# Moving the expert-row gathers of a transformer block along the routing: a pace for each of its five phases

## Chip, cores and metric

The kernel runs on one core of a Trainium2 chip. The metric is the device time of one execution in microseconds (us). The kernel before takes 3159.07 us in the median of 3 runs (3156.07 to 3160.61). The core has five engines with a queue each: PE (TensorE, matrix products), DVE (VectorE), ACT (ScalarE), POOL (GpSimd) and SP (SyncE, which here only issues DMAs). DMAs are issued by SP, ACT and POOL, each on a queue of its own (q1, q10 and q0 in the profile), and 16 DMA engines move the data of all of them.

## What is computed

The reference is two blocks on 512 tokens of width 1024, in float32. The part that matters here is the feed-forward of the first block, in which every token picks its experts out of 16384:

```
q  = (t @ wq) split into 8 heads x 2 halves of 128
s  = q . sub_keys                      # 8 heads x 2 x 128 scores per token
s1, i1 = top16(s[:, :, 0]);  s2, i2 = top16(s[:, :, 1])
cand = s1[:, None] + s2[None, :]       # 16 x 16 per head
top, pos = top16(cand);  idx = i1 * 128 + i2 at pos
g = softmax(top)
a = gelu(u[idx] . t)                   # 8 heads x 16 experts per token
out = sum over the 128 picks of (g * a) * v[idx]
```

Ahead of it stands a mixer (neighbourhood attention and a gated linear recurrence), and behind it the second block (short convolution, attention, two dense feed-forwards). Neither is touched.

## The kernel before

**Two ways through the feed-forward.** The 512 tokens are four tiles of 128. Tiles 1 to 3 (`dense`, 384 tokens) are computed over all 16384 experts, as 128 "experts" of 128 rows each: `hidden` makes `gelu(U_e . t)` for a whole e with 24 matmuls of 384 columns; `products` multiplies with V, 18 matmuls of 512 columns per e, after `operands` has multiplied the hidden values by the weights `Wr` that the routing gave (zero where an expert isn't picked). Tile 0 goes another way: its 128 picks per token are fetched row by row. A gather (L1135) is an indirect DMA that POOL issues: 128 rows of 1024 floats, one for each token, into a tile `gr`, of which there are five (`GBUFS`). For the tables U and V together there are 256 of them. On a row of U, DVE makes the dot product with the token (`gr`, L1154); on a row of V it adds weight times row to `accg` (L1157 once, then L1159). After 16 dot products ACT makes their gelu (L1161) and DVE the weights `wt` (L1162). A gather is issued `GAHEAD` = 3 gathers ahead of the row that DVE works on.

**The stage of the routing** (716 to about 1305 us). In `peer`, three lists of work are woven (L1046):

- `route`: in five phases. In phases 0 to 3 `topk` finds the top 16 for one token tile, on DVE alone (L1230 to L1234, L1271 to L1274). In phases 2 to 4 `spread` makes the dense weights of tiles 1 to 3: DVE compares (`oh`, `go`, L1313), ACT scales, PE multiplies the one-hots (`spread_mm`), ACT writes them out to `Wd` in DRAM. In phases 2 and 3 the two are merged.
- `ahead`: the hidden values of the first 112 experts, each with a load of U by SP, a split by ACT (`wh`, L1341) and DVE (`wl`, L1342), the 24 matmuls on PE, and a write of the result to `Ad` in DRAM. The other 4 of `AHEAD` = 116 follow behind the routing, the last 12 in the products.
- `until_routed(gather)`: once tile 0 has its experts (`choose`, at the end of phase 0), pairs of gathers. A pair is one of U and one of V from the second head on.

`weave` gives each list a clock of its own: what a list yields is the time in us that its last piece is taken to last, and the list whose clock is behind goes next. `route` yields 1.0 for a search, 1.45 for a piece of `spread` and so on, some 330 in all; `ahead` yields `PACE` = 2.95 an expert; a pair of gathers yields `GATHER` = 11.0 (L1164). PE's order is kept as woven (`manual_schedule`); the orders of the other engines come from the scheduler, which takes the woven order as its start. The rows on gathered tiles are placed behind the last search or spread piece woven so far (`self.after(self.anchor)`).

**The stage of the products with V** (about 1322 to 1960 us). What is left of the 129 pairs (`gather_left`, L1121), 103, is dealt out evenly to the first 120 experts (L1062 and following). For each expert SP loads V (`w`, L1374) and the hidden values (`act`, L1367), and once in 8 experts (`GROUP`) the weights `Wr` of eight experts (L1364, in runs of 512 bytes). DVE multiplies (`act`, L1371) and splits (`sl`, `vl`, L135), ACT splits (`sh`, `vh`, L133), and PE runs its 18 matmuls two experts behind (`OPS_LAG`). There are 3 tiles of `act`, 2 of `Wr` and 4 of `w`.

All engines work their queues in order. A row of DVE that waits for its gather holds everything behind it on DVE.

Of the kernel before, what the change touches and what calls it, by code (L numbers as in the profile page):

```python
# [29 lines left out]
WT = 16  # L30
GBUFS = 5
GAHEAD = 3
GATHER = 11.0
OPS_LAG = 2
TAIL = 2
STATE = 3.0
# [39 lines left out]
def merge(*gens):  # L76

    at = [[0.0, i, g] for i, g in enumerate(gens)]
    out = [None] * len(gens)
    while at:  # L80
        cur = min(at, key=lambda x: (x[0], x[1]))
        try:
            d = next(cur[2])
            cur[0] += d
            yield d
        except StopIteration as e:
            out[cur[1]] = e.value
            at.remove(cur)
    return out


class Net:
# [1030 lines left out]
    def gathered(self, pg, ac):  # L1123


        nc, p = self.nc, self.p
        iu, iv, g = self.chosen
        dots = ac.tile([128, 8, 16], F32, name="dots")
        wt = ac.tile([128, 8, 16], F32, name="wt")
        self.accg = acc = ac.tile([128, D], F32, name="accg")  # L1130
        ring = {}

        def load(key, table, idx):
            ring[key] = t = pg.tile([128, D], F32, name="gr", bufs=GBUFS)
            nc.gpsimd.indirect_dma_start(out=t, out_offset=None, in_=table, in_offset=bass.IndirectOffsetOnAxis(ap=idx, axis=0))  # L1135

        jobs = []
        for h in range(9):
            for k in range(16):
                if h < 8:  # L1140
                    jobs.append(("u", h, k))
                if h:
                    jobs.append(("v", h - 1, k))
        for n in range(len(jobs) + GAHEAD):
            if n < len(jobs):
                what, h, k = jobs[n]
                i = h * 16 + k
                load(n, p['Un'] if what == "u" else p['V'].rearrange("a b d -> (a b) d"), (iu if what == "u" else iv)[:, i:i + 1])
            if n >= GAHEAD:
                what, h, k = jobs[n - GAHEAD]  # L1150
                t = ring.pop(n - GAHEAD)
                with self.after(self.anchor):
                    if what == "u":
                        nc.vector.scalar_tensor_tensor(t, t, 1.0, self.h0, op0=OP.mult, op1=OP.mult,  # L1154
                                                       accum_out=dots[:, h, k:k + 1])
                    elif h == k == 0:
                        nc.vector.tensor_scalar(acc, t, wt[:, h, k:k + 1], None, op0=OP.mult)  # L1157
                    else:
                        nc.vector.scalar_tensor_tensor(acc, t, wt[:, h, k:k + 1], acc, op0=OP.mult, op1=OP.add)  # L1159
                if what == "u" and k == 15:  # L1160
                    nc.scalar.activation(wt[:, h], dots[:, h], AF.Gelu)  # L1161
                    nc.vector.tensor_tensor(out=wt[:, h], in0=wt[:, h], in1=g[:, h], op=OP.mult)  # L1162
            if n % 2:
                yield GATHER  # L1164

    def queries(self, mv, first):

# [31 lines left out]
    def route(self, pq, pg, sc):  # L1199
        nc = self.nc  # L1200
        self.io = io = pq.tile([128, 128], F32, name="io")
        nc.gpsimd.iota(io, pattern=[[1, 128]], base=0, channel_multiplier=0, allow_small_or_imprecise_dtypes=True)
        self.routing = True
        cur = None
        for t in range(5):
            gens = []
            if t < 4:
                gens.append(self.topk(pq, sc[t], io))
            if t > 1:
                gens.append(self.spread(pq, t - 1, *cur, io))  # L1210
            cur = (yield from merge(*gens))[0]
            if t == 0:
                self.choose(pg, *cur)
        self.routing = False
# [616 lines left out]
```

## Time and profile before

| | us |
|---|---|
| median of 3 runs | 3159.07 |
| range of the runs | 3156.07 to 3160.61 |
| the profiled execution, its own time | 3161.74 |
| its span in the trace | 3159.9 |

| engine | busy us | share of the span |
|---|---|---|
| PE | 2967.1 | 94% |
| DVE | 1900.2 | 60% |
| ACT | 1268.5 | 40% |
| POOL | 472.1 | 15% |

The DMA engines move 170 GB/s in the mean over the span. The shares are means over very different stages, so the profile is read stage by stage: for each stretch the busy time of each engine, the granted clock of PE (1.00 is its full speed of 2.4 GHz, the other level is 1.2 GHz), the mean busy share of the 16 DMA engines and what they moved. An engine whose busy time fills a stretch bounds it; DMA bounds it where its share stands at 1.0. Matmuls are pipelined, so the distance of their starts, not their own duration, is what one costs. The rows themselves follow in a section of their own.

### The profile page before, as it was taken

Reading aid. Unit: us, or ns where it says so; the run is one execution under the profiler, and the core shown is the slowest. Engines: PE = TensorE matmul, PEld = TensorE weight load, DVE = VectorE, ACT = ScalarE, POOL = GpSimd, SP = SyncE. Lnnn points to the kernel's source line nnn. Section 1 sums busy time; section 2 is a strip of 40 time slices with the busy share of each in tenths; the row PEclk is TensorE's granted clock in tenths of the full one; section 3 lists DMA queues with packets and bytes.
Section 4 is the critical chain, followed back from the end, with each engine's and each line's share of the span. In section 5 each row is a group of like instructions: output and inputs, shape, how many; then the busy total and the mean of one; then the engine's idle time right before and its main releaser. Section 6 shows DMA issues by size and latency. Waiting matters only on the chain.

```text
span 3159.9 us, 42417 instructions
## 1 busy us (share of the span) xinstructions
PE 2967.1 (94%) x16073; PEld 2540.5 (80%) x16073; DVE 1900.2 (60%) x3614; ACT 1268.5 (40%) x2275; POOL 472.1 (15%) x464
## 2 busy tenths in 40 slices
PE   7999889999999999898898888899999999999998
PEld 5887787799899999777776767778888887788887
DVE  5744487539999856588788885544333235533323
ACT  4233464343376677532223323432433234433222
POOL 2101332000111111043344441000000000000000
PEclk9999899999999999999999999999999999999999
DMA  6622202235766766799999996223333322133332
GB/s 245 230 61 75 62 1 71 97 114 162 233 218 235 252 229 234 270 356 365 356 348 349 365 360 225 67 74 97 94 96 94 100 87 68 48 92 95 94 106 80
DMA packets 257165, 537.79 MB, mean 170 GB/s; under 512 B 20160, under 2 KB 135104, under 8 KB 252608
## 3 DMA queue, kind: packets, MB, share of 16 engines
q1 hardware_dynamic: 196512, 345.82, 33.9%
q0 software_dynamic: 36864, 134.23, 12.1%
q10 hardware_dynamic: 23584, 55.03, 4.6%
q8 instruction: 126, 2.06, 0.3%
q14 instruction: 79, 0.65, 0.1%
HBM read 484.93 MB, written 50.08 MB: 169 GB/s over the span
## 4 chain that ended last, share of the span: by engine, by line
PE 58%; DVE 18%; DMA 8%; issue 3%; ACT 1%; POOL 1%; SPq 0%; DVEq 0%; ACTq 0%; POOLq 0%
PE bank L122 56%; DMA act<-Ad 6%; DVE wl L1342 2%; DVE accg L1159 2%; DVE gr L1154 2%; DVE vl L135 2%; DVE sl L135 1%; DVE act L1371 1%; PE bank L606 1%; PE bank L1470 1%; DVE idx L1274 1%; DVE tmp L1232 1%; DVE eq L1271 1%; DVE eq L1273 1%; DVE go L1313 1%
## 5 line engine op out<-in xcount | busy, mean ns | idle before, releaser
L122 PE MATMUL bank<-hh,wl 128*128 128x512 f32 (+2 forms) x2304 | 839.2, 365 | 45.9 <-DVE wl L1342 32.2
L122 PE MATMUL bank<-hh,wh 128*128 128x512 f32 (+2 forms) x2304 | 843.6, 367 | 15.1 <-ACT wh L1341 5.3
L122 PE MATMUL bank<-hl,wh 128*128 128x512 f32 (+2 forms) x2304 | 833.0, 362 | 1.1 <-DVE hl L272 0.6
L149 DVE TENSOR_TENSOR wl<-w,wh 128x1024 fp32r<-128x1024 f32 (+2 forms) x280 | 303.4, 1084 | 651.5 <-ACT wh L148 643.8
L148 ACT ACTIVATE wh<-w 128x1024 fp32r<-128x1024 f32 (+2 forms) x280 | 257.4, 920 | 751.7 <-PE bank L122 609.9
L122 PEld LDWEIGHTS bank<-hh,wl 128*128 128x128 f32 x2304 | 438.4, 190 | 106.0 <-DVE wl L1342 42.6
L122 PEld LDWEIGHTS bank<-hh,wh 128*128 128x128 f32 x2304 | 438.0, 190 | 66.7 <-ACT wh L1341 6.1
L122 PEld LDWEIGHTS bank<-hl,wh 128*128 128x128 f32 x2304 | 438.6, 190 | 50.5 <-DVE hl L530 1.4
L122 PE MATMUL bank<-vh,sh 128*128 128x512 f32 x768 | 249.6, 407 | 43.6 <-ACT sh L133 24.5
L1135 POOL DMA_INDIRECT gr<-in_Un_dram,iu x128 | 165.9, 1296 | 738.7 <-DVE accg L1159 496.6
L122 PE MATMUL bank<-vl,sh 128*128 128x512 f32 x768 | 251.6, 410 | 19.2 <-DVE vl L135 19.0
L122 PE MATMUL bank<-vh,sl 128*128 128x512 f32 x768 | 247.1, 404 | 0.0
L133 ACT ACTIVATE sh<-act 128x384 fp32r<-128x384 f32 x128 | 67.1, 525 | 383.0 <-DVE act L1371 346.5
L122 PEld LDWEIGHTS bank<-vh,sh 128*128 128x128 f32 x768 | 150.5, 198 | 79.3 <-ACT sh L133 27.4
L1342 DVE TENSOR_TENSOR wl<-w,wh 128x1024 fp32r<-128x1024 f32 x128 | 155.8, 1219 | 77.4 <-ACT wh L1341 77.4
L1341 ACT ACTIVATE wh<-w 128x1024 fp32r<-128x1024 f32 x128 | 134.9, 1055 | 165.1 <-PE bank L122 142.3
L122 PEld LDWEIGHTS bank<-vl,sh 128*128 128x128 f32 x768 | 150.7, 199 | 58.6 <-DVE vl L135 27.3
L122 PEld LDWEIGHTS bank<-vh,sl 128*128 128x128 f32 x768 | 151.3, 197 | 33.5 <-DVE sl L135 0.3
L1135 POOL DMA_INDIRECT gr<-in_V_dram,iv x128 | 150.2, 1174 | 175.7 <-DVE gr L1154 107.3
L216 POOL TENSOR_TENSOR r<-r,mhalf 128x1 f32<-128x1 f32 x37 | 21.8, 591 | 1026.5 <-DVE r L215 1019.8
L135 DVE TENSOR_TENSOR vl<-w,vh 128x1024 fp32r<-128x1024 f32 x128 | 156.3, 1221 | 12.7 <-ACT vh L133 12.3
L1159 DVE SCALAR_TENSOR_TENSOR accg<-gr,wt,accg 128x1024 f32<-128x1024 f32 x127 | 162.4, 1279 | 0.0
(375 smaller groups left out, 4889.8 us busy)
## 6 DMA issues: line engine op xcount, KB each, us to landing
w<-in_U_dram SPq DMA_DIRECT2D x128, 512.0 KB, 4.6
w<-in_V_dram SPq DMA_DIRECT2D x128, 512.0 KB, 7.1
w<-in_wgu_dram SPq DMA_DIRECT2D x84, 512.0 KB, 3.7
Wd<-W ACTq DMA_DIRECT2D x24, 1024.0 KB, 6.7
Wr<-Wd SPq DMA_DIRECT2D x16, 1536.0 KB, 17.9
w<-in_wdown_dram SPq DMA_DIRECT2D x44, 512.0 KB, 3.6
Ad<-act ACTq DMA_DIRECT2D x116, 192.0 KB, 3.8
act<-Ad SPq DMA_DIRECT2D x116, 192.0 KB, 6.8
```

The source lines that it names most:

```text
L122: return self.nc.tensor.matmul(out, a, b, start=start, stop=stop)
L133: self.nc.scalar.activation(hi, src, AF.Copy)
L135: (low or self.nc.vector).tensor_tensor(out=lo, in0=src, in1=hi, op=OP.subtract)
L148: self.nc.scalar.activation(hi[:, :, :n], w[:, :, :n], AF.Copy)
L149: (self.low or self.nc.vector).tensor_tensor(out=lo[:, :, :n], in0=w[:, :, :n], in1=hi[:, :, :n], op=OP.subtract)
L606: nc.tensor.matmul(o, x[k], y[:, kk, :256], start=k == 0 and i == 0 and t % 2 == 0, stop=k == KC - 1 and i == 2, skip_group_check=True)
L1135: nc.gpsimd.indirect_dma_start(out=t, out_offset=None, in_=table, in_offset=bass.IndirectOffsetOnAxis(ap=idx, axis=0))
L1154: nc.vector.scalar_tensor_tensor(t, t, 1.0, self.h0, op0=OP.mult, op1=OP.mult, accum_out=dots[:, h, k:k + 1])
L1159: nc.vector.scalar_tensor_tensor(acc, t, wt[:, h, k:k + 1], acc, op0=OP.mult, op1=OP.add)
L1232: nc.vector.match_replace(tmp, val[:, 0:8], src, -3e38)
L1341: nc.scalar.activation(uh, w, AF.Copy)
L1342: nc.vector.tensor_tensor(out=ul, in0=w, in1=uh, op=OP.subtract)
```

## The change

`GATHER` becomes a table of five numbers, one for each phase of `route`, and `route` writes the number of the phase that it is in to `self.phase`. A pair of gathers so counts 14.0 in phases 0 and 1 (in which none or the first of them run), 11.0 in phase 2, as before, 4.3 in phase 3 and 1.7 in phase 4.

```diff
-GATHER = 11.0
+GATHER = (14.0, 14.0, 11.0, 4.3, 1.7)
...
             if n % 2:
-                yield GATHER
+                yield GATHER[self.phase]
...
         self.routing = True
         cur = None
         for t in range(5):
+            self.phase = t
             gens = []
```

`gather_left` becomes 69 of 129 pairs, dealt out to the same 120 experts. No instruction is added or taken away. Two places show what moves; in both listings the names are those of the part above, and lines of the kernel after stand one number higher behind the added line.

DVE at the end of the routing, from the 102nd expert's `wl` to the next one, before:

```order
L1342 TENSOR_TENSOR wl<-w,wh 128x1024
L1313 TENSOR_TENSOR oh<-io,eT 128x512
L1313 TENSOR_TENSOR go<-io,eT 128x512
L1313 TENSOR_TENSOR oh<-io,eT 128x512
L1313 TENSOR_TENSOR go<-io,eT 128x512
L1159 SCALAR_TENSOR_TENSOR accg<-gr,wt,accg 128x1024
L1154 SCALAR_TENSOR_TENSOR gr,dots<-gr,h_5526 128x1024
L1313 TENSOR_TENSOR oh<-io,eT 128x512
L1342 TENSOR_TENSOR wl<-w,wh 128x1024
```

and after, between the same two:

```order
L1343 TENSOR_TENSOR wl<-w,wh 128x1024
L1159 SCALAR_TENSOR_TENSOR accg<-gr,wt,accg 128x1024
L1162 TENSOR_TENSOR wt<-wt,gw 128x16
L1154 SCALAR_TENSOR_TENSOR gr,dots<-gr,h_5526 128x1024
L1314 TENSOR_TENSOR oh<-io,eT 128x512
L1314 TENSOR_TENSOR go<-io,eT 128x512
L1159 SCALAR_TENSOR_TENSOR accg<-gr,wt,accg 128x1024
L1154 SCALAR_TENSOR_TENSOR gr,dots<-gr,h_5526 128x1024
L1314 TENSOR_TENSOR oh<-io,eT 128x512
L1314 TENSOR_TENSOR go<-io,eT 128x512
L1343 TENSOR_TENSOR wl<-w,wh 128x1024
```

Where one expert in four had a pair of rows on gathered tiles, an expert now has two to four such rows between its `wl` and the next.

DVE in the products, from the 62nd product of `act` and `Wr` on, before:

```order
L1371 TENSOR_TENSOR act<-act,Wr 128x384
L1159 SCALAR_TENSOR_TENSOR accg<-gr,wt,accg 128x1024
L135 TENSOR_TENSOR sl<-act,sh 128x384
L135 TENSOR_TENSOR vl<-w,vh 128x1024
L1154 SCALAR_TENSOR_TENSOR gr,dots<-gr,h_5526 128x1024
L1371 TENSOR_TENSOR act<-act,Wr 128x384
```

and after:

```order
L1372 TENSOR_TENSOR act<-act,Wr 128x384
L135 TENSOR_TENSOR sl<-act,sh 128x384
L135 TENSOR_TENSOR vl<-w,vh 128x1024
L1372 TENSOR_TENSOR act<-act,Wr 128x384
L1159 SCALAR_TENSOR_TENSOR accg<-gr,wt,accg 128x1024
L135 TENSOR_TENSOR sl<-act,sh 128x384
L135 TENSOR_TENSOR vl<-w,vh 128x1024
L1154 SCALAR_TENSOR_TENSOR gr,dots<-gr,h_5526 128x1024
L1372 TENSOR_TENSOR act<-act,Wr 128x384
```

Of the experts in the products nearly all had a pair, and now about two in three have one. PE's order in the routing is the same in both kernels.

## Rows read from the trace of the kernel before

**Rows 1.** the page, slices of 79 us: busy tenths of DVE and of DMA.

```profile
DVE  5744487539999856588788885544333235533323
...
DMA  6622202235766766799999996223333322133332
```

**Rows 2.** busy time by stage, all instructions; the first line names the columns.

```profile
core 0: us, PE busy (x) PEld busy (x) DVE busy (x) ACT busy (x) POOL busy (x), PEclk, DMA share, GB/s
715.80:1035.50 319.70, 301.48 (x1783) 294.73 (x1782) 318.49 (x1095) 171.33 (x301) 38.32 (x28) 0.99 0.65 213
1035.50:1115.10 79.60, 77.19 (x485) 76.13 (x484) 67.14 (x89) 55.97 (x114) 14.68 (x10) 1.00 0.75 253
1115.10:1196.90 81.80, 81.80 (x522) 81.80 (x521) 46.88 (x58) 57.89 (x110) 10.47 (x8) 1.00 0.74 250
1196.90:1304.50 107.60, 102.49 (x642) 97.18 (x641) 69.11 (x96) 87.47 (x194) 10.47 (x8) 1.00 0.63 220
...
1330.00:1900.00 570.00, 503.88 (x2048) 404.56 (x2049) 461.59 (x635) 165.40 (x227) 227.90 (x192) 0.92 1.01 357
```

**Rows 3.** the same stages, instructions of line L1342 alone, one for each expert.

```profile
715.80:1035.50 319.70, 77.71 (x64) 0.99 0.65 213
1035.50:1115.10 79.60, 18.24 (x15) 1.00 0.75 253
...
1196.90:1304.50 107.60, 19.50 (x17) 1.00 0.63 220
```

**Rows 4.** DVE in order of time: start us, us, instruction; 1127 to 1131 us.

```profile
1127.68 1.28 DVE L1159 SCALAR_TENSOR_TENSOR accg<-gr,wt,accg 128x1024 f32<-128x1024 f32 x1
1128.88 1.22 DVE L1154 SCALAR_TENSOR_TENSOR gr<-gr,h 128x1024 f32<-128x1024 f32 x1
1130.02 0.08 DVE L1154 DVE_READ_ACCUMULATOR gr<-gr,h 128x1 f32 x1
```

**Rows 5.** DMA queues from 1330 to 1900 us: packets, MB, share of 16 engines.

```profile
q0 software_dynamic: 27648, 100.68, 48.4%
```

**Rows 6.** SP's queue in order of time: start us, us to issue.

```profile
1516.93 0.38 SPq L1364 DMA_DIRECT2D Wr<-Wd  x1
1518.60 12.17 SPq L1367 DMA_DIRECT2D act<-Ad  x1
```

**Rows 7.** DVE in order of time; in brackets the idle time before and its releaser.

```profile
1537.92 0.56 DVE L1371 TENSOR_TENSOR act<-act,Wr 128x384 f32<-128x384 f32 x1 [8.24 <-DMA act<-Ad]
```

**Rows 8.** what DVE waited for, 1330 to 1900 us: us in total, times, longest.

```profile
DVE act L1371 <- DMA act<-Ad: 101.5, 16, 8.9
```

**Rows 9.** landing of `Wr`, from the view of that tile.

```profile
DMA to landing us min/median/max: 7.5/17.9/20.5
```

**Rows 10.** PE in order of time around one of these waits.

```profile
1534.16 0.62 PE L122 MATMUL bank<-vl,sh 128*128 128x512 f32 x2
1534.61 0.61 PE L122 MATMUL bank<-vh,sl 128*128 128x512 f32 x2
1539.14 0.73 PE L122 MATMUL bank<-vh,sh 128*128 128x512 f32 x2 [3.92 <-ACT sh L133]
...
1541.16 1.05 PE L122 MATMUL bank<-vh,sh 128*128 128x512 f32 x2
1542.01 1.05 PE L122 MATMUL bank<-vl,sh 128*128 128x512 f32 x2
```

**Rows 11.** gathers (L1135) over the span: duration ns min/median/max, and landing.

```profile
L1135 POOL DMA_INDIRECT gr<-in_Un_dram,iu x128: 939/1014/2149, 781.2 to 1874.7; - x128
...
DMA to landing us min/median/max: 4.1/7.3/10.2
```

**Rows 12.** the page, DMA issues: count, KB each, median us to landing.

```profile
w<-in_V_dram SPq DMA_DIRECT2D x128, 512.0 KB, 7.1
...
Wr<-Wd SPq DMA_DIRECT2D x16, 1536.0 KB, 17.9
...
act<-Ad SPq DMA_DIRECT2D x116, 192.0 KB, 6.8
```

## The prediction, as it went on record

> **What bounds the kernel now.** I read the forty slices first, then the busy time by stage, then the rows inside the two stages that the change touches. In the slices [rows 1] DVE is near 9 in the tenth to fourteenth slice, and DMA stands at 9 from the eighteenth to the twenty-fourth. So the routing and the products with V, one behind the other, have different limits. The table by stage [rows 2] cuts the routing where the 1st, 65th, 80th and 96th expert's `wl` comes (counts in [rows 3]; one record seems to be missing there, so a boundary may be off by one expert).
>
> - 716 to 1036 us (64 experts): DVE is busy 318.49 of 319.70 us. It is full; PE gets 301 us of work done beside it, so it only just waits. DMA is at 0.65.
> - 1036 to 1115 us (16 experts): DVE 67.14 of 79.60, PE 77.19. DVE has 12.5 us left.
> - 1115 to 1197 us (16 experts): PE is full, DVE has 34.9 us left, DMA stands at 0.74.
> - 1197 to 1304.5 us (16 experts, with the last token tile's one-hots, 64 `oh` and `go` rows): PE 102.49 of 107.60; DVE has 38.5 us left and DMA 0.37 of the stretch. This is the loosest place of the routing.
> - 1330 to 1900 us, the products: DMA is busy 1.01 of the time at 357 GB/s, PE 504 of 570 at a granted clock of 0.92, DVE 462. DMA is the bound.
>
> The rows inside the products say how the full DMA reaches PE. SP issues the next `Wr` (1536 KB [rows 12], once in 8 experts) at 1516.9 us, and the `act` behind it takes 12.17 us to issue [rows 6]. DVE, done at 1529.7, stands until 1537.9 for that `act` [rows 7]. There are 16 such waits, 101.5 us in all [rows 8]. Their source is the landing of `Wr`, 17.9 us in the median [rows 9, 12] but 7.5 at best [rows 9]: it queues behind other traffic. PE, two experts behind, then stops for 3.92 us and afterwards runs at the lower of its two clock levels: two matmuls 0.85 us apart instead of 0.45 [rows 10].
>
> **The change part by part.** PE's order in the routing stays as it was. Only the gathers move. Counted in the two orders of DVE, its rows on gathered tiles are, before and after: ahead of the 65th expert's `wl` 23 and 24; up to the 81st 10 and 22; up to the 97th 8 and 19; up to the 113th 8 and 52; behind that 207 and 139. Each such row is one gather of 128 rows of 4 KB (0.524 MB) on POOL's queue and one pass of DVE. The passes cost 1.20 and 1.14 us from start to start [rows 4], 1.17 us in the mean.
>
> *A gather's price on the DMA engines.* In the products POOL's queue q0 took 48.4% of 16 engines' 570 us [rows 5] for the 192 gathers that POOL issued there [rows 2]: 275.9 / 192 = 1.44 us of all engines for one.
>
> *The products.* 68 gathers leave; 192 of 207 fall into the stretch, so 63 of them there, 63 x 1.44 = 91 us of DMA. The DMA work of the stretch goes from 1.01 x 570 = 576 us to 485. PE has 2048 matmuls [rows 2] at 0.455 us for two [rows 10], 466 us: still under 485, so DMA stays the bound, with only 4% between the two. DVE, at 462, loses 63 x 1.17 = 74. Bounds: 485 if DMA stays full (-85); 466 if PE alone set the end (-104); 538 if only some 40% of the DMA relief is used, because the `Wr` comes in bursts and DMA then idles between them (-32). I take 500, that is DMA busy 97% of the time, because with 0.91 of the time asked for between the bursts there is little room for idling: an expert takes 0.52 MB of V, 0.20 of `act` [rows 12] and 1.15 gathers (138 over 120 experts), 1.32 MB in eighteen matmuls' 4.1 us, or 324 of the 357 GB/s. **-70 us.**
>
> *Routing up to the 81st expert.* 13 gathers more on DVE, 13 x 1.17 = 15.2 us, against 1.2 + 12.5 = 13.7 us that DVE had free. At least 1.5 us is lost. At most all 15, as the order also puts a part of the last search some six experts later (its end moves from the 78th `wl` to the 84th; what it feeds is transposed by PE ahead of the 97th, so that wait isn't reached). I take **+5**. The 'few beside the first searches' is worth nothing on balance: 24 against 23 rows by the 65th expert.
>
> *81st to 97th expert.* 11 gathers more: 12.9 us of DVE against 34.9 free, 15.8 us of DMA against 0.26 x 81.8 = 21.3 free. **0**; if the cover is gone, up to 15.
>
> *97th to 113th expert.* 44 gathers more. DVE: 69.1 + 44 x 1.17 = 120.6 us against a stretch of 107.6, so +13 from DVE alone. DMA: 0.63 x 107.6 = 67.8, plus 44 x 1.44 = 63.4, makes 131 us, +23.6. DMA becomes the bound, at the very place where the loosest stretch was. Behind a late gather DVE's in-order queue holds the `wl` of the next expert, for which PE waits, and `oh`/`go`, for which PE's one-hot products wait. I take DMA's figure and a little for gathers that come late although DMA is full: **+25**, between +13 and +63 (rival B). This stretch gives back part of what the products gain.
>
> *What is beside it.* The last experts, the 12 whose first product is made late, see 5 gathers less or more at most: 0. SP's own list of loads is the same, in nearly the same order. POOL had 38.32 us of work in 319.7 in the densest DVE stretch, 1.37 us a gather [rows 2]; 52 of these are 71 us in a stretch of 131.
>
> *Sum.* -70 + 5 + 0 + 25 = -40 us. The profiled execution took 3161.7 us, so 3121.7 there; that run lies 2.7 us above the median of the runs shown, 3159.07, so I forecast **3119 us**.
>
> **A rule weighed.** In the stretch where DVE was full a gather took POOL 1.37 us, in the products 1.19 [rows 2], and the longest on U's table 2.15 [rows 11]: the issue does get slower beside a busy DVE, and the crowded stretch has DVE busy throughout. What a slow issue costs there is worked out from these rows as rival B. The Trainium skill, SBUF — State Buffer, section 'SBUF: two separate sides', says that DMAs issued from GpSimd's queue are starved while DVE runs certain operations, since the descriptors can't be written through the locked port; its example grows from about 620 to 3100 ns. By that figure the 52 gathers of the crowded stretch would keep POOL busy for an estimated 161 us, the stretch would cost 53 us in place of 25, and the kernel would end near 3147. The trace shows the direction of that rule, but no gather on U's table as slow as its example.
>
> **The rivals.**
>
> *A. The waits for `Wr` are a matter of lead, not of load (slower).* SP is about three `act` ahead of DVE, 12.8 us from the issue of `Wr` (1516.9) to the point at which DVE needs it (1529.7). If `Wr` and the `act` behind it still land some 18 us later, the same stop stands at each group of 8 experts, PE runs 8 x 4.1 = 33 us and stops as before, and the products give back nothing. Then only the routing's cost is left: +30, **3189 us**. It decides against the change as soon as less than 30 of the 91 us come back, that is if a group of 8 (about 41 us) shortens by under 2 us. For it: these waits sit at one place per group. Against it: `Wr` can land in 7.5 us, and DMA's 1.01 leaves no doubt that it queues.
>
> *B. The five buffers of the gather ring set the pace of the crowded stretch (no change).* A buffer's round is the pass on DVE, the issue and the landing; with the longest in the trace, 1.28 [rows 4] + 2.15 + 10.2 us [rows 11], a round is 13.6 us, 2.7 us a gather, 141 us for 52. While DVE stands for one it does none of its other 60 us (`wl` and one-hot rows: 69.1 of [rows 2] less 8 gathers' 9.4); if half of that isn't hidden, the stretch takes 171, +63. With -70 and +5: -2, **3157 us**. Against it: the medians, 1.01 and 7.3 us, give 1.9 us a gather, 100 us.
>
> *C. DMA stays full and nothing else is lost.* Products -85, crowded stretch +13 since writes of `Wd` and `Ad` can lag, the rest 0: -72, **3087 us**.
>
> That the change doesn't do what it says can be set aside: the order shows 52 gathers where 8 were, and 139 behind.
>
> **How the numbers follow.** The forecast's own case 0.62 (it runs from 3089, products -85 and routing +15, to 3149, products -55 and routing +45), A 0.12, B 0.08, C 0.18. About 0.2% (6 us) is what a measurement of this kernel can tell from no change. Faster by more: 0.62 + 0.18 = 0.80; within: 0.08; slower: 0.12. The range goes from below C, at 3070 (products at PE's 466 us, -104, with +13 to +15 in the routing), up to 3158 with B, and leaves A out.
>
> **What would show it.** In the new profile: the stretch of the last 16 experts of the routing grows from 107.6 to some 130 us, with DMA at 0.95 or more and DVE waiting for gathers; DVE's waits on `act<-Ad` in the products fall from 101.5 us to under 50, the median landing of `Wr` falls from 17.9 us to under 15, the granted clock of the products rises above 0.92, and the stage takes about 500 us. The prediction is wrong if the products keep their stops of some 40 us spacing (A), if the crowded stretch takes over 150 us (B), or if it isn't longer at all (then the sum lacks a cover that I don't see).

## The result, and the profile after

The change makes the kernel slower. It takes 3240.27 us in the median (3233.27 to 3256.14), the kernel before 3159.84 in the same comparison (3156.07 to 3161.09): 1.026 times as long, 95% interval 1.0231 to 1.0288. The forecast was 3119 us; the sign is wrong. The profiled execution, the fastest of its four, has a span of 3231.2 us, 71.3 more than before.

The forty slices of the page, DVE and DMA, answer to [rows 1]:

```profile
DVE  5744396549999879766666666544433235543323
...
DMA  6622102236676789988878888313233231123332
```

DMA stood at 9 through the products with V before. Now it stands at 8: no engine is full in them, and still they take longer. The table by stage says the same in numbers. Each stretch runs from the start of one expert's `wl` to that of another (1st, 65th, 81st, 97th, 113th), the last from the 9th to the 113th product of `act` and `Wr`. The columns are those of [rows 2]. After:

```profile
692.10:1022.20 330.10, 313.52 (x1898) 306.83 (x1896) 314.41 (x1081) 179.28 (x316) 38.37 (x30) 0.99 0.63 209
1022.20:1125.00 102.80, 90.02 (x518) 88.07 (x519) 89.81 (x159) 61.20 (x118) 28.74 (x20) 0.92 0.73 253
1125.00:1207.30 82.30, 79.73 (x508) 79.41 (x508) 64.61 (x87) 56.01 (x109) 29.01 (x21) 1.00 0.86 312
1207.30:1336.00 128.70, 110.09 (x651) 104.36 (x650) 119.17 (x161) 91.51 (x195) 66.28 (x52) 0.95 0.97 368
...
1387.90:1971.20 583.30, 486.62 (x1940) 384.23 (x1939) 366.27 (x495) 155.25 (x216) 140.90 (x121) 0.93 0.83 276
```

The same stretches of the kernel before, without the first one:

```profile
1024.80:1112.50 87.70, 85.30 (x521) 84.23 (x522) 75.83 (x104) 59.51 (x118) 14.68 (x10) 0.98 0.73 243
1112.50:1191.50 79.00, 79.00 (x505) 79.00 (x504) 46.88 (x58) 56.02 (x108) 10.47 (x8) 1.00 0.73 248
1191.50:1303.30 111.80, 106.69 (x666) 101.38 (x666) 69.18 (x95) 89.22 (x196) 10.47 (x8) 1.00 0.64 223
...
1358.10:1890.60 532.50, 469.72 (x1903) 376.32 (x1903) 430.60 (x589) 156.63 (x215) 213.68 (x180) 0.92 1.01 357
```

The routing costs 35 us more (15 + 3 + 17), about what was forecast. The products, from which 70 us were to go, cost 51 us more. DVE has 64 us less to do there and moves less data (276 GB/s in place of 357). What DVE waits for in that stretch, after (total us, times, longest), and PE:

```profile
DVE act L1372 <- DMA act<-Ad: 212.5, 81, 9.4
...
PE bank L122 <- DVE vl L135: 96.6, 45, 5.4
```

What SP's queue waits for, from 1380 to 1960 us, in the same columns:

```profile
SPq L1368 <- DVE sl L135: 292.7, 82, 8.7
```

The same of the kernel before, from 1358 to 1890 us:

```profile
SPq L1367 <- DVE sl L135: 162.8, 54, 11.2
```

In [rows 8] DVE waited 16 times, 101.5 us in all; 12 of these waits, 91 us, stand at the third expert of a group of eight, whose `act` SP issues right behind a `Wr`. Now it waits at four experts out of five: 89 us at the first expert of a group, where the `act` behind a `Wr` now stands, and 124 us at the other seven. In both kernels DVE's work and its waits for `act` make up nearly the whole stretch: 430.6 + 101.5 of 532.5 us before, 366.3 + 212.5 of 583.3 after. So the change took 64 us of work from DVE there and gave it 111 us of waiting. Yet the loads themselves have become quicker. The landing of `Wr`, from that tile's view, against [rows 9]; and the page's DMA issues, against [rows 12]:

```profile
DMA to landing us min/median/max: 7.8/10.0/13.6
```

```profile
w<-in_V_dram SPq DMA_DIRECT2D x128, 512.0 KB, 5.3
...
act<-Ad SPq DMA_DIRECT2D x116, 192.0 KB, 4.8
```

`Wr` lands in 10.0 us in place of 17.9, V in 5.3 in place of 7.1, `act` in 4.8 in place of 6.8. So the `act` is not slow, it is asked for too late, and SP's row says why: SP waits for DVE's `sl`. It did so before too, but then the load still left well ahead of its use. A tile of `act` is free when its last reader, `sl`, is done; there are three tiles, so the load for expert k + 3 can't go out before the `sl` of expert k. One such load in time, after, DVE's queue and then SP's:

```profile
1508.86 0.55 DVE L135 TENSOR_TENSOR sl<-act,sh 128x384 fp32r<-128x384 f32 x1
...
1512.01 0.56 DVE L1372 TENSOR_TENSOR act<-act,Wr 128x384 f32<-128x384 f32 x1 [0.33 <-DMA act<-Ad]
1512.49 0.55 DVE L135 TENSOR_TENSOR sl<-act,sh 128x384 fp32r<-128x384 f32 x1
...
1518.26 0.56 DVE L1372 TENSOR_TENSOR act<-act,Wr 128x384 f32<-128x384 f32 x1 [4.09 <-DMA act<-Ad]
```

```profile
1509.43 0.33 SPq L1368 DMA_DIRECT2D act<-Ad  x1
...
1513.07 0.33 SPq L1368 DMA_DIRECT2D act<-Ad  x1
```

The `sl` ends at 1509.41, the load leaves at 1509.43, and the very next product, at 1512.01, is the one that needs it. The next `sl` ends at 1513.04, the load leaves at 1513.07, and DVE stands 4.09 us for it. The same place before:

```profile
1509.08 0.55 DVE L135 TENSOR_TENSOR sl<-act,sh 128x384 fp32r<-128x384 f32 x1
...
1511.93 0.56 DVE L1371 TENSOR_TENSOR act<-act,Wr 128x384 f32<-128x384 f32 x1
...
1516.35 0.56 DVE L1371 TENSOR_TENSOR act<-act,Wr 128x384 f32<-128x384 f32 x1
...
1520.76 0.56 DVE L1371 TENSOR_TENSOR act<-act,Wr 128x384 f32<-128x384 f32 x1
```

```profile
1509.66 0.32 SPq L1367 DMA_DIRECT2D act<-Ad  x1
```

Here the load of 1509.66 serves the third product behind it, at 1520.76: a lead of 11 us in place of 2.6. These two are typical: matched load by load from the 9th to the 113th product, the time from the issue of an `act` to the point at which DVE is ready for it is 11.0 us in the median before and 2.6 after. The difference stands in DVE's order. With the numbers of the tiles, at the place that the section on the change showed without them, before (left out: the rows on gathered tiles and `vl`):

```
L1371 TENSOR_TENSOR act_15206<-act_15206,Wr_15025 128x384
L135 TENSOR_TENSOR sl_15211<-act_15206,sh_15209 128x384
L1371 TENSOR_TENSOR act_15243<-act_15243,Wr_15025 128x384
L135 TENSOR_TENSOR sl_15248<-act_15243,sh_15246 128x384
```

and after:

```
L1372 TENSOR_TENSOR act_15310<-act_15310,Wr_15135 128x384
L135 TENSOR_TENSOR sl_15241<-act_15236,sh_15239 128x384
L1372 TENSOR_TENSOR act_15341<-act_15341,Wr_15135 128x384
L135 TENSOR_TENSOR sl_15278<-act_15273,sh_15276 128x384
L1372 TENSOR_TENSOR act_15378<-act_15378,Wr_15135 128x384
L135 TENSOR_TENSOR sl_15315<-act_15310,sh_15313 128x384
```

Before, a product is followed by its own `sl`. After, the `sl` of `act_15310` stands behind the products of the next two experts. Counted over the 128 experts: before, 118 `sl` stand behind their own product and 10 behind the next one; after, 16, 42 behind the next and 70 behind the one after that. Each place that `sl` falls back is a tile of lead lost, and with two of three lost a load goes out only just ahead of its use.

### The profile page after: what moved, and what is told of

It is laid out like the page before. It is cut to its first block, busy times and chain, and to the rows that moved or that the text cites. A ratio compares the mean times of both kernels' runs of the same rounds, so it can differ in the third digit from the quotient of the medians.

```text
span 3231.2 us, 42528 instructions
## 1 busy us (share of the span) xinstructions
PE 2984.2 (92%) x16073; PEld 2551.6 (79%) x16073; DVE 1904.6 (59%) x3614; ACT 1267.6 (39%) x2275; POOL 473.1 (15%) x464
## 4 chain that ended last, share of the span: by engine, by line
PE 52%; DVE 18%; DMA 14%; issue 4%; POOL 1%; ACT 1%; SPq 0%; DVEq 0%; POOLq 0%; ACTq 0%
PE bank L122 50%; DMA act<-Ad 10%; DVE accg L1159 3%; DMA gr<-in_Un_dram,iu 2%; DVE wl L1343 2%; DVE gr L1154 2%; DVE sl L135 1%; DVE vl L135 1%; DVE oh L1314 1%; PE bank L606 1%; PE bank L1471 1%; DVE go L1314 1%; DMA Ad<-act 1%; DVE KX L801 1%; DVE QX L802 1%
## 5 line engine op out<-in xcount | busy, mean ns | idle before, releaser
L1135 POOL DMA_INDIRECT gr<-in_Un_dram,iu x128 | 174.0, 1360 | 732.1 <-DVE accg L1159 472.7
L1372 DVE TENSOR_TENSOR act<-act,Wr 128x384 f32<-128x384 f32 x128 | 71.1, 559 | 227.4 <-DMA act<-Ad 220.8
L1342 ACT ACTIVATE wh<-w 128x1024 fp32r<-128x1024 f32 x128 | 135.1, 1056 | 166.6 <-PE bank L122 145.9
L1135 POOL DMA_INDIRECT gr<-in_V_dram,iv x128 | 149.6, 1169 | 245.8 <-DVE accg L1159 138.1
L216 POOL TENSOR_TENSOR r<-r,mhalf 128x1 f32<-128x1 f32 x37 | 21.8, 590 | 1028.4 <-DVE r L215 1021.6
```

The source lines that it names most:

```text
L1342: nc.scalar.activation(uh, w, AF.Copy)
L1372: self.anchor = nc.vector.tensor_tensor(out=a3, in0=a3, in1=self.Wr[:, :, e % GROUP], op=OP.mult)
```

## Experiments

**Theory O** (order): fewer gathers on DVE in the products let the scheduler put products of later experts ahead of an `sl`; this takes the lead from the loads of `act` and is the whole of the loss. One rival is that the moved gathers themselves cost it, by a fuller routing and by what they leave in the products. The other, L, puts the waits down to `Wr` and a short lead of SP, whatever the order. Later questions were whether the stops that stayed at the groups of eight are a matter of lead (L again) or of load (Q), and which of the moved gathers pay.

All stretches below are cut as in the tables above: "routing" from the 1st to the 113th `wl`, "products" from the 9th to the 113th product. The kernel before has 608.8 and 532.5 us, after 643.9 and 583.3.

**One edit that restores the order, in both kernels.** Each product is put behind the `sl` of the expert before; nothing else.

```diff
-        self.anchor = nc.vector.tensor_tensor(out=a3, in0=a3, in1=self.Wr[:, :, e % GROUP], op=OP.mult)
-        sh, sl = self.split(pm, a, [128, TD], "s", bufs=TAIL + OPS_LAG)
+        with (self.after(self.last_sl) if e else ExitStack()):
+            self.anchor = nc.vector.tensor_tensor(out=a3, in0=a3, in1=self.Wr[:, :, e % GROUP], op=OP.mult)
+        sh = pm.tile([128, TD], FR, name="sh", bufs=TAIL + OPS_LAG)
+        nc.scalar.activation(sh, a, AF.Copy)
+        sl = pm.tile([128, TD], FR, name="sl", bufs=TAIL + OPS_LAG)
+        self.last_sl = nc.vector.tensor_tensor(out=sl, in0=a, in1=sh, op=OP.subtract)
```

In the kernel after:

> The kernel after, with one constraint more: on DVE the product of act and Wr of an expert comes behind the subtraction sl of the expert before it, as it mostly stood in the kernel before. The gathers stay where the change put them (139 behind the routing). Theory O (order): the products lost their lead because the new order of DVE puts sl of an expert behind the products of the next one or two, and with three act tiles the next load then starts only when it is needed. By it the waits of DVE for act fall from 209 us to under 80, the products take about 500 us in place of 610 and the kernel some 3120 to 3145 us. Rival L (lead): the waits belong to Wr and to the short lead of SP whatever the order; then this kernel stays within 1% of the kernel after, about 3240 us.

Measured: 3121.41 us (3117.16 to 3123.74), 0.9882 of before [0.9863, 0.9902]. In the kernel before:

> The kernel before with the same constraint on DVE's order. There only a dozen of the 128 sl stood behind the next product, so theory O expects no change that can be measured, 3150 to 3165 us. Rival L expects the same. It is the control for the constraint itself.

Measured: 3147.26 us (3143.61 to 3151.45), 0.9963 [0.995, 0.9977], 3 us under what was expected: the order has a price in the kernel before too, though only 10 `sl` were late there. The products, of before with the edit and of after with it, and DVE's wait in the latter:

```profile
1358.70:1884.60 525.90, 465.98 (x1912) 373.78 (x1911) 429.87 (x588) 156.96 (x215) 216.43 (x180) 0.93 1.01 361
```

```profile
1398.60:1858.50 459.90, 440.83 (x1906) 360.79 (x1906) 360.38 (x495) 156.52 (x213) 191.36 (x120) 0.99 0.98 344
```

```profile
DVE act L1373 <- DMA act<-Ad: 86.9, 20, 8.1
```

With the order kept, the same gathers moved bring the products from 525.9 to 459.9 us. DVE's waits are 86.9 us, a little over the 80 expected, in place of the 212.5 of after: 126 us less, and the stretch is 123 us shorter. The routing is as dear as in after (651.8 against 643.9). So the loss of after is the order, and neither the moved gathers nor L; theory O holds for the kernel after.

**More tiles of `act`.** If a lost lead is the trouble, tiles should buy it back: six in place of three, the order left to the scheduler.

```diff
...
-            a = pm.tile([128, TD], F32, name="act", bufs=3)
+            a = pm.tile([128, TD], F32, name="act", bufs=6)
...
```

> The kernel after with six act tiles in the products in place of three, nothing else written differently. By theory O the load of act gets its lead back, whatever the order: DVE's waits for act under 60 us, products at or below 500 us, 3110 to 3140 us in all. By rival L, SP still issues Wr just ahead of its use and each group of eight experts keeps its stop: 3200 to 3240 us.

Measured: 3210.81 us (3209.48 to 3217.09), 1.0166 [1.0149, 1.0184]. This was a miss for O, and the time lies in the range that rival L gave. The products take 556.3 us, and DVE still waits in them (9th to 113th product):

```profile
DVE act L1372 <- DMA act<-Ad: 187.5, 50, 10.2
```

The order tells why: with six tiles 104 of the 128 `sl` stand behind products three to five experts later. The scheduler runs the products as far ahead as the tiles allow, and little of the added lead is left for the loads: the median from issue to DVE's being ready is 3.9 us, against 2.6 in after and 11.0 before. L's own reason does not hold, since a `Wr` is issued some 45 us ahead of its first use (see below).

**The late `sl` alone, in the kernel before.** The gathers stay, every `sl` is put behind the product two experts later.

```diff
+            if e >= OPS_LAG:
+                ops[e - OPS_LAG] = self.late_split(pm, ops[e - OPS_LAG])
...
+    def late_split(self, pm, ops):
+
+        a, sh, vh, vl = ops
+        sl = pm.tile([128, TD], FR, name="sl", bufs=TAIL + OPS_LAG)
+        with self.after(self.anchor):
+            self.nc.vector.tensor_tensor(out=sl, in0=a, in1=sh, op=OP.subtract)
...
```

> The kernel before, its gathers untouched (207 of them behind the routing), with the subtraction sl of an expert put behind the product of act and Wr of the expert two later, for all experts. By theory O this order alone costs: every load of act is then waited for (a landing of 3 to 6 us for each of 116 experts), 3200 to 3280 us. By rival L the order alone costs nothing that can be measured, 3150 to 3170 us.

Measured: 3323.65 us (3309.62 to 3327.5), 1.051 [1.0481, 1.054]. The routing is as before (611.9 us), the products take 682.2, with DMA at 0.84 and 276 GB/s, as in after. It is dearer than expected, and two rows of 1400 to 1840 us show that it isn't the loads of `act` alone:

```profile
PE bank L122 <- DVE sl L1386: 115.4, 56, 7.7
DVE act L1373 <- DMA act<-Ad: 79.7, 45, 7.0
```

PE waits for the late `sl` itself. So this run shows that a late `sl` is dear without any gather moved, not how much of it is the lead.

**A few gathers moved.** No constraint, paces (11, 11, 11, 11, 4.3): 20 gathers in the last 16 experts of the routing in place of 8, and 195 left in place of 207.

```diff
-GATHER = (14.0, 14.0, 11.0, 4.3, 1.7)
+GATHER = (11.0, 11.0, 11.0, 11.0, 4.3)
```

> The kernel after without any constraint on DVE's order, and with the paces (11, 11, 11, 11, 4.3), so that only 12 gathers move into the last 16 experts of the routing (20 there where before has 8; 195 behind). In the scheduled order of DVE 84 of 128 products then have their sl behind the product of a later expert (80 by one, 4 by two), where before has 10 and after 112. Theory O (the order of sl is what costs): the products get slower although 12 gathers leave them, between -12 and +50 us, and the kernel is not faster than before: 3160 to 3200. Theory G (the order costs only together with the other moves): the products -12, the routing +2, the kernel 3145 to 3152.

Measured: 3170.35 us (3163.13 to 3175.64), 1.0034 [1.0022, 1.0047]. The routing is at 611.9, the last 16 experts of it at 111.9 (before 111.8): these 12 gathers are hidden there. The products grow to 547.4 us although 12 gathers have left them. The kernel and the products lie in O's ranges; G falls. In the orders, 84 `sl` are late here, 112 in after, 10 in before.

**Lead or load at the groups of eight.** In the code each `Wr` is asked for six experts earlier, besides the kept order.

```diff
-        if e % GROUP == 0:
-            self.Wr = pm.tile([128, TD // WT, GROUP, WT], F32, name="Wr", bufs=2)
-            nc.sync.dma_start(self.Wr, self.Wd[:, :, e:e + GROUP, :].rearrange("b p e t -> p b e t"))
+        if e % GROUP == 0 and e:
+            self.Wr = self.next_Wr
+        if e == 0 or (e % GROUP == 2 and e + GROUP - 2 < 128):
+            g = 0 if e == 0 else e + GROUP - 2
...
```

In the kernel after:

> The kernel after, with each product act x Wr kept behind the sl of the expert before (as in e1_in_turn), and besides that each group's Wr issued six experts earlier (behind the second expert of the group before). In e1 the stretch from the 9th to the 113th product took 459.9 us, with 86.9 us in which DVE stood for an act (20 times) although PE stood only for 19.1. Theory L (the stops at the group boundaries are a matter of lead: the act behind Wr lands late because Wr is issued just ahead of it): DVE's waits for act fall under 30 us, the stretch to some 440 us, since PE has 1906 matmuls there at 0.455 us for two, 434 us; the kernel takes 3095 to 3108. Theory Q (the load of DMA alone makes them late, wherever Wr is issued): the waits only move, 70 us or more of them stay, the stretch takes 455 to 465 and the kernel 3115 to 3128.

Measured: 3118.96 us (3116.33 to 3125.67), 0.9873 [0.9849, 0.9897]: no different from the 0.9882 without it. In the kernel before:

> The same two edits in the kernel before (gathers untouched). Its products with the first edit took 525.9 us, with DMA busy 1.01 of a 460 us stretch at 363 GB/s, and DVE standing 87.1 us for act (13 times). Theory Q, and also L as far as DMA has nothing left to give: the stretch stays within 515 to 530 us and the kernel within 3138 to 3152, whatever the lead. If lead were all, the stretch would fall to PE's 440 to 460 us and the kernel to 3075 or so, and the gathers' share of DMA would cost the products nothing: rival A of the prediction.

Measured: 3145.58 us (3140.1 to 3156.92), 0.9969 [0.9954, 0.9985], as without it. DVE's waits in the former, 1400 to 1840 us:

```profile
DVE act L1380 <- DMA act<-Ad: 93.5, 23, 9.1
```

Both times lie in Q's ranges, but the pair does not decide between L and Q, because the edit moved hardly any load. SP's queue in the kernel after in turn, and then with the edit:

```profile
1532.97 0.33 SPq L1368 DMA_DIRECT2D act<-Ad  x1
1533.44 0.38 SPq L1365 DMA_DIRECT2D Wr<-Wd  x1
1537.39 3.32 SPq L1368 DMA_DIRECT2D act<-Ad  x1
```

```profile
1532.64 0.33 SPq L1375 DMA_DIRECT2D act<-Ad  x1
1533.11 0.38 SPq L1368 DMA_DIRECT2D Wr<-Wd  x1
1537.05 5.03 SPq L1375 DMA_DIRECT2D act<-Ad  x1
```

In the orders of all four kernels in turn, from the third `Wr` on, a `Wr` stands behind the `act` of the second expert of the group before its own, with the edit or without it; the second `Wr` alone was moved. With two tiles of `Wr` it can't go out much earlier: its tile is free only when the group two before its own has had its last product. From the issue of a `Wr` to the first product of its group pass 38.2 us in the median without the edit and 38.6 with it, and in the kernel before in turn 44.0 and 43.5. So DVE's waits did not move either: 73 of 87 us without the edit and 75 of 93.5 with it stand at the third expert of a group, whose `act` SP issues right behind the `Wr`. That a `Wr` of 1536 KB holds up the `act` behind it is what these rows show; whether it would cost less in another place, or in smaller pieces, was not tried.

**Which of the gathers pay.** The order kept, and only the last stretch crowded (40 gathers in it, 175 left):

```diff
+GATHER = (11.0, 11.0, 11.0, 11.0, 2.0)
```

> The kernel after with the product kept in turn as in e1_in_turn, and the paces (11, 11, 11, 11, 2.0): the first four phases as before, only the last one crowded, 40 gathers in the last 16 experts of the routing where before had 8 and after has 52, and 175 behind instead of 139. If routing and products are two separate sums: the routing up to the 97th expert costs 0, the last 16 experts some +16 (e1: 44 gathers more for +21.9), the products -32 (e1: 68 gathers less for 526 - 460 = 66 us); the kernel 3147 - 16 = 3131, 3124 to 3138. If the crowded stretch has a fixed price for being DMA-bound at all, it is +22 and the kernel 3137.

Measured: 3138.06 us (3131.87 to 3140.32), 0.9938 [0.9914, 0.9962]. Only the two stretches ahead of it fuller, as in after (22 and 19 gathers; 183 left):

```diff
+GATHER = (14.0, 14.0, 11.0, 4.3, 11.0)
```

> As e7_turn_crowd_only with the paces (14, 14, 11, 4.3, 11): the middle phases of after, 22 and 19 gathers up to the 81st and the 97th expert where before has 10 and 8, and the last stretch as before with 8; 183 behind. Two separate sums: +18 to +20 for the 65th to the 97th expert (e1: +20.5 against the kernel before in turn), 0 in the last 16 experts, -24 in the products; the kernel 3141 to 3146, so that these 24 gathers bring next to nothing. If the cost of the middle in after comes from the later end of the routing's searches and not from DVE's time, it also shows here in full; if it came from buffers held by the crowd behind, it is under +8 and the kernel is at 3130.

Measured: 3146.02 us (3142.53 to 3150.06), 0.9958 [0.9946, 0.9969]. The crowded stretch of the first, and the 65th to the 81st expert of the second:

```profile
1191.00:1309.40 118.40, 107.03 (x659) 101.99 (x659) 105.25 (x145) 89.41 (x193) 53.44 (x40) 0.97 0.91 338
```

```profile
1019.20:1121.80 102.60, 89.76 (x518) 87.82 (x519) 89.84 (x159) 62.09 (x119) 28.76 (x20) 0.91 0.73 254
```

Against the kernel before in turn, 32 gathers in the last stretch cost it 6.5 us (118.4 - 111.9) and bring the products 22.7 (525.9 - 503.2), where 32 were expected. The 23 gathers in the middle cost 21 us (102.6 + 85.1 against 87.6 + 79.0) and bring 23.5: nothing is left. Neither expectation for the crowded stretch, 16 or 22 us, was right, and that kernel's time, at the edge of the range, hides two errors that cancel; the one for the middle was right within some 1 us.

**A faster kernel.** So the middle is left alone and the last stretch crowded further (54 gathers in it, 161 left), the order kept:

```diff
+GATHER = (11.0, 11.0, 11.0, 11.0, 1.5)
```

> As e7_turn_crowd_only with the last pace at 1.5 in place of 2.0: 54 gathers in the last 16 experts of the routing (e7: 40; after: 52), the middle as before with 10 and 8, and 161 behind (e7: 175; after: 139). In e7 the last stretch cost +6.5 us for 32 gathers more and the products gave back 22.7. If the next 14 follow the products' mean of 1.0 us a gather and the stretch is by now DMA-bound at 1.44 us each: -14 +15 to +20, the kernel stays at 3132 to 3142 and e1_in_turn remains the fastest. If the stretch still hides them: 3118 to 3128, as fast as e1 or faster with 29 gathers less moved in the middle.

Measured: 3116.48 us (3106.7 to 3124.87), 0.9879 [0.9853, 0.9904]. The crowded stretch and the products:

```profile
1183.50:1316.30 132.80, 114.83 (x680) 108.41 (x678) 121.92 (x166) 92.11 (x197) 70.79 (x53) 0.95 0.95 357
1371.10:1840.30 469.20, 444.02 (x1901) 361.77 (x1900) 382.58 (x524) 155.57 (x214) 198.62 (x139) 0.98 1.02 358
```

Both expectations were half right, and the time is a little under both ranges. The 14 gathers more cost the last stretch 14.4 us, 1 us each, so little of them is hidden by then; but the products gave back 34 (503.2 to 469.2), more than 1 us each. That makes it as fast as the first experiment, with fewer gathers moved; the two can't be told apart, and both are 1.2% faster than the kernel before. Of this the kept order alone gives the kernel before 0.4%.

## Why the prediction was wrong

**The step that failed** is the sentence "SP's own list of loads is the same, in nearly the same order", and behind it "DMA stays the bound" in the products. SP's list is the same, but when a load leaves is set by DVE's `sl`, and DVE's order had changed. In its place the runs showed this: 112 `sl` instead of 10 stand behind a later product, DMA is busy for only 0.83 of the stretch, DVE stands 212.5 us for `act` in place of 101.5, and the products cost 51 us more instead of 70 less. The listing of DVE's order in the section on the change held this and hid it: without tile numbers, "product, `sl`, `vl`" reads alike whether the `sl` belongs to that product or to one two experts earlier. I took the rows as showing only fewer gathers. None of the rivals had it either. A comes nearest, since lead it was; but it looked for the lost lead at one `Wr` in eight experts, not at each `act`. It also misread the rows: the `Wr` issued at 1516.9 us serves the group whose first product starts at 1562.3, 45 us later, and what DVE stood for at 1529.7 was the `act` queued behind it. And its conclusion does not follow: with the order kept these stops stay (73 us in the products), and yet the products give back 66 us.

**Where the order is kept, the sum stands nearly as forecast.** Stretches in us, from the profiled executions:

| | before | before in turn | after in turn | after |
|---|---|---|---|---|
| to the 1st `wl` | 694.5 | 691.1 | 691.6 | 692.1 |
| 1st to 65th | 330.3 | 331.9 | 330.8 | 330.1 |
| 65th to 81st | 87.7 | 87.6 | 102.0 | 102.8 |
| 81st to 97th | 79.0 | 79.0 | 85.2 | 82.3 |
| 97th to 113th | 111.8 | 111.9 | 133.8 | 128.7 |
| to the 1st product | 19.1 | 20.1 | 22.0 | 21.8 |
| 1st to 113th product | 568.2 | 563.0 | 493.1 | 613.4 |
| to the 128th | 126.8 | 118.3 | 118.4 | 116.3 |
| the rest | 1142.5 | 1142.5 | 1142.3 | 1143.6 |
| span | 3159.9 | 3145.4 | 3119.2 | 3231.1 |

- *The products, -70:* right in size with the order kept, 563.0 to 493.1, that is -69.9; and the reason (DMA relief, then PE close behind: 440.83 of 459.90 us busy at 0.99 of its clock) is seen in the windows. Without the order it is +45, from 568.2 to 613.4.
- *97th to 113th, +25:* +17 in after, +22 with the order kept, with DMA at 0.97 and 368 GB/s as forecast. DMA was taken for the bound from 1.44 us a gather; 32 gathers more cost only 6.5 us, and only from 40 to 54 did each cost 1 us. Whether DMA or DVE sets the length there is not separated: DVE is busy 119.17 of 128.70 us, and it waits 5.4 us in all for gathers.
- *65th to 81st, +5, the term that was mis-sized:* +15. DVE got 14 us more work (75.83 to 89.81) and was idle as long as before (11.9 us, then 13.0). I had set the new work against that idle time, but none of it was used up: the new rows bring waits of their own, and 8.8 of the 13.0 us are DVE's for two late gathers (2.5 before). The next 16 experts, at 0, came to +3 to +6.

The two rows for PE's wait in that stretch, before and after:

```profile
PE bank L122 <- DVE wl L1342: 4.1, 3, 2.0
```

```profile
PE bank L122 <- DVE wl L1343: 13.9, 5, 5.7
```

- *First 64 experts and the last ones, 0:* right with the order kept (118.3 and 118.4 us to the 128th product). The kernel before takes 8.5 us more for the latter than with its own order kept.
- *The sum, -40:* the kernel after with the order kept is 39.8 us under the kernel before (3121.41 against 3161.22 in that comparison). This agreement is partly luck: 14 of these come from the constraint itself, which the kernel before gets too. The paces alone are worth 26 (3147.26 to 3121.41), -70 and +43.
- *The rule weighed:* the 52 gathers of the crowded stretch kept POOL busy for 66.28 us, 1.27 each; the 8 of the same stretch before took 10.47 us, 1.31 each. The gathers on U's table in it, before and after:

```profile
L1135 POOL DMA_INDIRECT gr<-in_Un_dram,iu x4: 1677/1679/1679, 1206.6 to 1286.6; - x4
L1135 POOL DMA_INDIRECT gr<-in_Un_dram,iu x26: 936/1677/1776, 1219.5 to 1335.2; - x26
```

The median is 1.68 us in both, so the crowd made no issue slower. Nor do the prediction's own rows show that a busy DVE does: from 1115 to 1197 us, with DVE busy for 46.88 of 81.80 us, a gather took 1.31 us too (10.47 for 8, [rows 2]). The Trainium skill, SBUF — State Buffer, section 'SBUF: two separate sides', says that a DMA issued from GpSimd's queue waits for its descriptors while DVE runs an operation in a 2-port mode. By its example, beside a `tensor_copy` on DVE, the 66 us would be an estimated 161. No run here shows that, and nearly all of DVE's work in the stretch is TENSOR_TENSOR and SCALAR_TENSOR_TENSOR, not copies. Rival B, built on slow issues, did not come.

**The signs named ahead.** The last stretch grew to 128.7 us with DMA at 0.97, and the landing of `Wr` fell under 15: both as written, in a kernel that was slower. DVE's waits for gathers there, also named, were 5.4 us. DVE's waits for `act` (212.5 us in place of under 50) and the length of the products showed it wrong, and the sign of rival A came too: the stops at the groups of eight stayed, 89 us in all. The signs on the load of DMA were right and said nothing on the time.

**What stays open.** Why the scheduler brings the products forward wasn't tried. Its orders alone, without a run, show a trend: with 207, 203, 195, 183, 175 and 139 gathers left behind the routing, 10, 57, 84, 100, 107 and 112 of the `sl` are late. That the room on DVE does it is likely and only argued. Lead against load at the groups of eight is open, as said above. Of the 34 us that 14 gathers fewer brought the products in the last experiment, 17 are DVE's work (399.38 to 382.58 us) and most of the rest shorter waits for `act` (83.3 to 60.3 us); why these got shorter isn't settled, and the profiled execution there, 3106.70 us, is the fastest of its four, 10 us under their median.

## What to carry to other kernels

When a change takes work from an engine whose order a scheduler makes, read the new order of that engine with its buffer numbers: ask for each tile which instruction frees it, and how many others now stand ahead of that one. A buffer's lead is the distance from the last reader to the load's use, not the number of tiles; more tiles don't bring it back if the scheduler spends them, one constraint on the order does. In the same way an experiment that moves a load in the code tests nothing until the scheduled order shows that the load has moved. And idle time in a stretch is room for more work only if it lies where that work can stand: 14 us of work added to a stretch with 12 us idle made it 15 us longer.

## What the runs showed besides

- The products moved 15% less data (583.3 us at 276 GB/s against 532.5 at 357), the loads landed faster (17.9 to 10.0 us for `Wr`), and DVE waited twice as long for them (101.5 to 212.5 us). Here landing times told nothing of lateness; the time from issue to use did (11.0 us in the median before, 2.6 after).
- In the crowded stretch DMA moved 368 GB/s at a busy share of 0.97, more than the 357 at 1.01 in the products, which have the `Wr` in runs of 512 bytes. Whether these runs are the reason wasn't tried.
- Taking 12 gathers out of the products made them 15 us longer (532.5 to 547.4), with 84 late `sl` in place of 10. That the order is the cause there is inferred from the other runs; this kernel wasn't run with the order kept.
